# Two decoder layers on one core: the main products read their moving operand in blocks of 16 columns, last block first

## The chip, the cores and the metric

The kernel runs on one core of one Trainium2 chip. Its time is the device time of one execution in microseconds (us). Of the kernel before, three executions were timed: 1609.34, 1609.86 and 1611.76 us, median 1609.86 us.

## What is computed

Two layers of a causal decoder over 256 tokens of 1024 features, in float32. Each layer has a feed-forward half step, a group of parallel mixers, and a second feed-forward half step; a norm ends the whole.

```python
for l in range(DEPTH):
    h = _rmsnorm(x, ffn1_norm[l])
    x = x + 0.5 * _swiglu(h, ffn1_w_gate[l], ffn1_w_up[l], ffn1_w_down[l])
    h = _rmsnorm(x, mix_norm[l])
    hq, hf, hi, hg, s5_in, conv_in, att_in, gate_in = split(h @ w_in[l])
    y_a, y_b, y_c, y_d = hgrn2(...), s5(...), conformer_conv(...), dilated_attention(...)
    merged = sum_k sigmoid(gate_k) * (y_k @ w_branch[l, k])
    x = x + merged @ w_out[l]
    h = _rmsnorm(x, ffn2_norm[l])
    x = x + 0.5 * _swiglu(h, ffn2_w_gate[l], ffn2_w_up[l], ffn2_w_down[l])
return _rmsnorm(x, final_norm)
```

The weights of the large products (`w_gate`, `w_up`, `w_down`, `w_in`, `w_branch`, `w_out`, `s5_w_glu`) are float32 as well.

## The kernel before

**Products in three parts.** Every large product runs in the type float32r. Both factors are split exactly into a high and a low part: ScalarE copies the value into a float32r tile (`whi`, `hTh`, `gh`, ...), VectorE subtracts it from the value (`wlo`, `hTl`, `gl`, ...). `mm3` then adds three products into one bank of PSUM: high by high, high by low and low by high. All large products of the kernel go through `mm3`, and nothing else does; transposes, attention scores and the recurrences call `T.matmul` or `T.transpose` directly.

**What is stationary and what moves.** In the call `T.matmul(o, ah, bh)` the first factor is loaded into the array (a weight load of 128 columns), the second moves through it, and `o` is the output in PSUM. In `cols_tok` and in the down product the activations are stationary (128 tokens) and 512 columns of weights move: 512 columns a product. In `cols_feat` and `rows_feat` 128 columns of weights are stationary and the activations of all 256 tokens move: 256 columns a product. The moving operand is always a contiguous run of one partition's row, and so is the output.

**Shares of the work.** A down product accumulates over 22 blocks of 128 rows, the products of `cols_tok` and `cols_feat` over 8, those of `rows_feat` over 4. Four banks (`acc`) take the accumulations in turn; four others (`mx`) serve transposes and side work.

**Order.** Weights come by `Stream` in the order of their use: SyncE loads them into `raw` (4 buffers), ScalarE makes `whi`, VectorE `wlo` (5 slots ahead). Side work (the recurrences, attention, convolution, tables) is a list of generators, of which `tick` runs steps between the main products when the class `Paced` estimates that the engines have room. The estimate counts the elements of an access, `math.prod(ap.shape[1:])`, and so does not depend on how they are ordered. Every engine's call passes through one line of `Paced` (L72), so the profile gives line 72 for all of them, and the tiles tell the products apart: `gate_h`, `up_h`, `pgt_h`, `pu_h`, `pf_h`, `pq_h`, `pa_h`, `pb_h`, `br` and `glu` have 256 moving columns, `down`, `att_t`, `gate_t`, `up_t`, `po_t`, `pi_t` and `pg_t` have 512. `hl` and `as` are side work in plain float32 (the first recurrence, attention scores).

Of the kernel before, what the change touches and what calls it, by code (L numbers as in the profile page):

```python
# [28 lines left out]
NW, NRAW = 5, 4                # buffers of the weights' low parts (one more of the high ones), of their loads  # L29
NHEAP, NHALF = 23, 10          # working tiles of 4 KB and of 2 KB a partition  # L30
TAIL, LAST = 5, 2              # weights of a down product that are held for the other tokens; by halves of the columns
EARLIER, HELD = 1, 1           # how long before a phase's end the first tokens' rows are turned, loads are left alone
GO = -1
HOP, EARLY = 0.15, -0.3        # from one engine to another; how soon before its operands are there a step is issued
LAG, TABLE_LAG, LAST_LAG = 3.8, 2.0, 1.8   # how far side work, tables, convolution may put an engine behind
# [7 lines left out]
class Paced:  # L43
    """An engine's instructions, with an estimate of when each of them ends: in order, after the
    other engines' work on the same tiles."""
# [40 lines left out]

SETS = {AF.Exp: 1, AF.Tanh: 1, AF.Silu: 2, AF.Sin: 2, AF.Sigmoid: 3, AF.Ln: 4, AF.Gelu_apprx_tanh: 5}


class ActCost:  # L90
    """With the loads of the functions' tables."""
# [22 lines left out]
class Stream:  # L114
    """Weights in the order of their use: loads, then an exact split into two 12-bit parts.

    A group is (loads, slots): loads are (source, blocks of 128 rows), slots (load, view -> part of it)."""
# [36 lines left out]
    def pump(self, n=1, ahead=True):  # L154
        """The low part of a slot whose high part is there, then the high part of the next."""
        for _ in range(n):
            self.load()
            if self.n_high == self.n_split:
                self.high()
            if self.n_high == self.n_split or self.n_split - self.n_done >= NW:  # L160
                return
            i, src, hv = self.half
            lo = self.pool.tile([P, 1024], FR, tag="wlo", name=f"wlo{self.n_split}", bufs=NW)
            lv = lo.rearrange("p (k f) -> p k f", k=src.shape[1])
            self.dve.tensor_tensor(lv, src, hv.bitcast(F32), op=ALU.subtract)
            self.ready.append((hv, lv))
            self.n_split += 1
            self.left[i] -= 1
            if not self.left[i]:
                del self.raw[i]  # L170
            self.load()
            if ahead:
                self.high()
# [15 lines left out]
def trunk(ctx, tc, x_in, positions, ffn1_norm, ffn1_w_gate, ffn1_w_up, ffn1_w_down, mix_norm, w_in,  # L189
# [44 lines left out]
    def g_tok(w, pieces, n_loads=2):  # L234
        """512 columns in 2 or 4 loads; slots of 256 rows."""
        loads = []
        k = 8 // n_loads
        for i in range(n_loads):
            parts, at = [], 0
            for c0, n in pieces:  # L240
                parts.append((rows_of(w, P * k * i, P * k, c0, n), at, n))
                at += n
            loads.append((parts, k))
        groups.append((loads, [(i, lambda r, j=j: r[:, 2 * j:2 * j + 2, :]) for i in range(n_loads)
                               for j in range(k // 2)]))

    def g_feat(w, c0, n=512):
        """n columns; slots of 512 rows and 256 columns."""
        if n == 512:
            loads = [([(rows_of(w, 512 * i, 512, c0, 512), 0, 512)], 4) for i in range(2)]  # L250
            groups.append((loads, [(i, lambda r, j=j: r[:, :, 256 * j:256 * j + 256])
                                   for j in range(2) for i in range(2)]))
        else:
            loads = [([(rows_of(w, 0, 1024, c0, 256), 0, 256)], 8)]
            groups.append((loads, [(0, lambda r, j=j: r[:, 4 * j:4 * j + 4, :]) for j in range(2)]))

    def g_rows_feat(w, order):
        """512 rows, 1024 columns; slots of all rows and 256 columns, given by the first columns of their halves."""
        for h in range(2):
            (a, b), (c, d) = order[2 * h:2 * h + 2]  # L260
            cols = [a, b, c, d]
            parts = []
            i = 0
            while i < 4:
                j = i + 1
                while j < 4 and cols[j] == cols[j - 1] + 1:
                    j += 1
                parts.append((rows_of(w, 0, 512, P * cols[i], P * (j - i)), P * i, P * (j - i)))
                i = j
            groups.append(([(parts, 4)], [(0, lambda r, j=j: r[:, :, 256 * j:256 * j + 256]) for j in range(2)]))  # L270
# [24 lines left out]
    def by_head(pieces):  # L295
        """Pairs of heads' pieces: (pair, which of it, head, kind, first group, number of pairs)."""
        a = 0
        while a < len(pieces):
            k, h, g = pieces[a]
            n = 2 if a + 2 < len(pieces) and pieces[a + 2][0] == k else 1  # L300
            for e in range(2):
                yield a // 2, e, h + e, k, g, n
            a += 2 * n
# [28 lines left out]
    side = []  # L332

    def start(gen, late=0):
        """late: done after the others. A step ends with GO where the next one waits for no other engine."""
# [28 lines left out]
    def grab(n=1):  # L364
        """Banks of the side work's own, held over several steps."""
        while free[0] < n:
            yield
        free[0] -= n
# [47 lines left out]
    # rows of 128 features, turned into columns of scalars  # L416
# [45 lines left out]
    def masks():  # L462
        # the attention's masks: d = t - s
# [14 lines left out]
    def prepare():  # L478
        # the recurrence's masks: s in the left block whose right neighbour has t
# [10 lines left out]
        # columns  # L490
# [22 lines left out]
        # rotary tables  # L513
# [8 lines left out]
        # cos(a) = sin(pi/2 - |reduced a|)  # L522
# [11 lines left out]
        # the gates' lower bounds: softmax over the two layers, less its first part  # L534
# [13 lines left out]
        # S5: the discretized states of both layers, 128 states a column  # L548
# [24 lines left out]
        # mag - 1, by tanh where it is small  # L573
# [31 lines left out]
    # S5 of a layer: blocks of 4 tokens, t = 4 n + i; groups of 16 channels G = 16 jp + 2 jh + g,  # L605
    # states on partitions (g, p) and columns j = 8 jp + jh, a block's inputs on partitions (jp, i, c)
# [5 lines left out]
    def s5_tables(l):  # L612
# [15 lines left out]
        # powers of the states' factors  # L628
# [23 lines left out]
        # the discretized inputs' matrices  # L652
# [8 lines left out]
        # a block's inputs to its last state  # L661
# [26 lines left out]
        # the outputs' matrices, for each token of a block  # L688
# [23 lines left out]
        # a block's inputs to its outputs: K_s = Re(C a^s b) for a distance of s tokens, and d at 0  # L712
# [46 lines left out]
    def s5_turns(l):  # L759
# [5 lines left out]
        # e^{4 i theta n} by doubling  # L765
# [32 lines left out]
    def mm3(o, ah, al, bh, bl, first, last):  # L798
        T.matmul(o, ah, bh, start=first, stop=False)
# [3 lines left out]
    def cols_tok(hT, evac, name, outer=False, between=None, before_last=None, at=4, mid=True):  # L803
        """512 columns, tokens on partitions; outer: all of the first 128 tokens, then the others."""
# [44 lines left out]
    def cols_feat(hT, evac, name, n=512, quiet=False):  # L849
        """n columns on partitions, all tokens: evac(half, bank) with two blocks of 128 columns a bank."""  # L850
# [17 lines left out]
    def rows_feat(yT, evac, name):  # L868
        """1024 columns on partitions from 512 inputs: evac(i, bank), two blocks of 128 columns a bank."""
# [24 lines left out]
    class Norm:  # L894
        """The rows of a norm, turned into hT; the first tokens' before the last ones are there."""
# [9 lines left out]
        def square(self, t, h):  # L905
            """A half of the columns of x."""
# [111 lines left out]
    class Tail:  # L1018
        """What follows the last product of a phase: x += scale * acc, and the next norm."""
# [15 lines left out]
    def mixers(l, norm, tail, g_tab):  # L1035
# [131 lines left out]
        def s5():  # L1167
# [5 lines left out]
            # channel (q, h, c) of rows (h, c): q = 2 jp + a, and group 8 a + h of jp  # L1173
# [49 lines left out]
            # the blocks' last states, turned back  # L1223
# [99 lines left out]
        def rope_turn(raw, pieces, name):  # L1323
            """The first 32 of each head's 128 are rotated, then the heads turned onto partitions."""
# [45 lines left out]
        def attend(h):  # L1370
# [5 lines left out]
            for qb in range(2):  # L1376
# [34 lines left out]
                # probabilities onto key partitions  # L1411
# [220 lines left out]
```

## Time and profile before

| | |
|---|---|
| three timed executions | 1609.34, 1609.86, 1611.76 us |
| profiled execution, first to last instruction | 1609.4 us |
| TensorE busy | 1583.1 us, 98% |
| weight loads (beside the products) | 1442.8 us, 90% |
| VectorE busy | 1109.6 us, 69% |
| ScalarE busy | 837.6 us, 52% |
| moved by DMA | 282.48 MB, mean 176 GB/s |

The profiled execution spans 1609.4 us, 0.5 us below the median of the timed ones. Matmuls are pipelined: a record of a product begins when the one before it is still running, so the busy time of one record is longer than the distance from one start to the next. How fast a run of products goes is therefore read from the chain of waits in order of time, where a run of products is one row with its length and its count. The granted clock stands at full speed in all 40 slices of the page.

### The profile page before, as it was taken

What the parts mean: (1) busy time and instruction counts of PE and PEld (TensorE: products, weight loads), DVE (VectorE), ACT (ScalarE), POOL (GpSimd) and SP (SyncE); (2) the same over time, 40 slices, a digit from 0 to 9 for tenths busy, and PEclk for the clock granted to TensorE, in tenths of its full rate; (3) what the DMA queues carried; (4) which work ended last, traced back from release to release, by engine and by line L of the source; (5) the groups of instructions that cost most, each with busy time, mean ns of one, the idle gap of its engine ahead of it and who ended that gap; (6) DMA issues with size and microseconds to landing.
All of it is one profiled execution on the core that took longest, in us unless ns stands there. A gap on an engine that the chain in (4) does not pass through costs nothing.

```text
span 1609.4 us, 27748 instructions
## 1 busy us (share of the span) xinstructions
PE 1583.1 (98%) x11471; PEld 1442.8 (90%) x11471; DVE 1109.6 (69%) x1806; ACT 837.6 (52%) x1195; POOL 23.9 (1%) x53
## 2 busy tenths in 40 slices
PE   7999999999999999999999999999999999999998
PEld 6999788789899997999889988987899999989986
DVE  6778865876778866555478774567867898665553
ACT  5445455557565465444345544646565555654442
POOL 1000000000000000000000000000000000000000
PEclk9999999999999999999999999999999999999999
DMA  8565556444444456555555545664444545645551
GB/s 278 185 177 210 171 186 191 154 141 148 147 168 158 159 186 219 184 175 207 181 173 187 184 161 193 206 194 119 170 131 148 190 161 168 212 158 184 185 212 61
DMA packets 179519, 282.48 MB, mean 176 GB/s; under 512 B 26718, under 2 KB 82080, under 8 KB 179392
## 3 DMA queue, kind: packets, MB, share of 16 engines
q1 hardware_dynamic: 154240, 270.55, 49.7%
q10 hardware_dynamic: 24832, 9.97, 2.7%
q8 instruction: 90, 1.47, 0.4%
q14 instruction: 37, 0.30, 0.1%
q0 software_dynamic: 320, 0.18, 0.0%
HBM read 277.53 MB, written 3.15 MB: 174 GB/s over the span
## 4 chain that ended last, share of the span: by engine, by line
PE 94%; ACT 2%; DVE 2%; ACTq 1%; issue 1%; DMA 0%; SPq 0%; POOLq 0%; POOL 0%; DVEq 0%
PE down L72 15%; PE att_t L72 12%; PE up_h L72 12%; PE gate_h L72 12%; PE pgt_h L72 11%; PE br L72 6%; PE gate_t L72 3%; PE po_t L72 3%; PE up_t L72 2%; PE hl L72 2%; PE pi_t L72 1%; PE pa_h L72 1%; PE pb_h L72 1%; PE pg_t L72 1%; PE pq_h L72 1%; PE pf_h L72 1%
## 5 line engine op out<-in xcount | busy, mean ns | idle before, releaser
L72 DVE TENSOR_TENSOR wlo<-raw,whi 128x1024 fp32r<-128x1024 f32 x512 | 614.7, 1220 | 185.7 <-ACT whi L72 85.4
L72 ACT ACTIVATE whi<-raw 128x1024 fp32r<-128x1024 f32 x512 | 525.5, 1053 | 175.9 <-PE down L72 102.7
L72 PE MATMUL gate_h<-hTh,wlo 128*128 128x256 f32 x576 | 161.0, 280 | 2.8 <-DVE wlo L72 2.8
L72 PE MATMUL up_h<-hTh,wlo 128*128 128x256 f32 x576 | 160.9, 279 | 0.8 <-DVE wlo L72 0.8
L72 PE MATMUL gate_h<-hTh,whi 128*128 128x256 f32 x576 | 161.6, 280 | 0.0
L72 PE MATMUL up_h<-hTh,whi 128*128 128x256 f32 x576 | 161.1, 280 | 0.0
L72 PE MATMUL gate_h<-hTl,whi 128*128 128x256 f32 x576 | 160.4, 278 | 0.0
L72 PE MATMUL up_h<-hTl,whi 128*128 128x256 f32 x576 | 160.3, 278 | 0.0
L72 PE MATMUL pgt_h<-hTh,whi 128*128 128x256 f32 x512 | 145.6, 284 | 0.0
L72 PE MATMUL pgt_h<-hTh,wlo 128*128 128x256 f32 x512 | 142.6, 278 | 0.0
L72 PE MATMUL pgt_h<-hTl,whi 128*128 128x256 f32 x512 | 142.5, 278 | 0.0
L72 PE MATMUL down<-whi,gh 128*128 128x512 f32 x352 | 140.0, 398 | 0.0
L72 PE MATMUL down<-wlo,gh 128*128 128x512 f32 x352 | 139.2, 395 | 0.0
L72 PE MATMUL down<-whi,gl 128*128 128x512 f32 x352 | 139.1, 395 | 0.0
L72 PE MATMUL att_t<-whi,hTh 128*128 128x512 f32 x288 | 118.2, 410 | 0.0
L72 PE MATMUL att_t<-wlo,hTh 128*128 128x512 f32 x288 | 113.8, 395 | 0.0
L72 PE MATMUL att_t<-whi,hTl 128*128 128x512 f32 x288 | 113.8, 395 | 0.0
L72 PEld LDWEIGHTS gate_h<-hTh,wlo 128*128 128x128 f32 x576 | 108.1, 188 | 3.2 <-DVE wlo L72 3.2
L72 PEld LDWEIGHTS up_h<-hTh,wlo 128*128 128x128 f32 x576 | 108.1, 188 | 1.0 <-DVE wlo L72 1.0
L72 PEld LDWEIGHTS gate_h<-hTl,whi 128*128 128x128 f32 x576 | 108.3, 188 | 0.0
L72 PEld LDWEIGHTS up_h<-hTl,whi 128*128 128x128 f32 x576 | 108.3, 188 | 0.0
L72 PEld LDWEIGHTS up_h<-hTh,whi 128*128 128x128 f32 x576 | 107.8, 187 | 0.2
(375 smaller groups left out, 3357.7 us busy)
## 6 DMA issues: line engine op xcount, KB each, us to landing
raw<-in_w_in_dram SPq DMA_DIRECT2D x60, 1024.0 KB, 5.1
raw<-in_ffn_w_up_dram SPq DMA_DIRECT2D x44, 1024.0 KB, 5.2
raw<-in_ffn_w_down_dram SPq DMA_DIRECT2D x44, 1024.0 KB, 4.9
raw<-in_ffn_w_gate_dram SPq DMA_DIRECT2D x42, 1024.0 KB, 5.1
raw<-in_w_in_dram SPq DMA_DIRECT2D x72, 512.0 KB, 4.5
raw<-in_w_branch_dram SPq DMA_DIRECT2D x16, 1024.0 KB, 5.0
raw<-in_w_out_dram SPq DMA_DIRECT2D x8, 1024.0 KB, 5.0
raw<-in_s_w_glu_dram SPq DMA_DIRECT2D x16, 256.0 KB, 3.8
```

The lines of the kernel that those rows point to most:

```text
L72: return f(*args, **kw)
```

## The change

`mm3` passes its output and its two moving operands through a new function, `backwards`. It replaces the last dimension of an access (n columns, step 1) by two: n/16 blocks with a step of -16 columns, beginning at column n-16, and in each block 16 columns with step 1. The same columns meet the same output columns; the order over the columns is the last 16 in rising order, then the 16 before them, and so on. The stationary operands are as before. The rest of the diff takes out comments and docstrings; the line of `Paced` that all calls pass stays line 72.

```diff
+def backwards(ap):
+
+    dims = [list(d) for d in ap.ap]
+    step, n = dims[-1]
+    assert step == 1 and n % 16 == 0
+    return bass.AP(tensor=ap.tensor, offset=ap.offset + n - 16, ap=dims[:-1] + [[-16, n // 16], [1, 16]])
...
     def mm3(o, ah, al, bh, bl, first, last):
+        o, bh, bl = backwards(o), backwards(bh), backwards(bl)
         T.matmul(o, ah, bh, start=first, stop=False)
         T.matmul(o, ah, bl, start=False, stop=False)
         T.matmul(o, al, bh, start=False, stop=last)
```

On TensorE's queue the products keep their places. Before, in the first feed-forward phase (a gate product with 256 columns, then the change of weights from one slot to the next):

```order
L72 MATMUL gate_h_741<-hTl_0_113,whi_583 128x256
L72 MATMUL gate_h_741<-hTh_0_111,wlo_626 128x256
L72 MATMUL gate_h_741<-hTh_1_112,whi_628 128x256
L72 MATMUL gate_h_741<-hTl_1_114,whi_628 128x256
L72 MATMUL gate_h_741<-hTh_1_112,wlo_657 128x256
```

And the same place now:

```order
L72 MATMUL gate_h_741<-hTl_0_113,whi_583 128x16x16
L72 MATMUL gate_h_741<-hTh_0_111,wlo_626 128x16x16
L72 MATMUL gate_h_741<-hTh_1_112,whi_628 128x16x16
L72 MATMUL gate_h_741<-hTl_1_114,whi_628 128x16x16
L72 MATMUL gate_h_741<-hTh_1_112,wlo_657 128x16x16
```

Nothing has moved; each product has two dimensions of 16 where it had one of 256. The second place is where the mixers' first projections begin (`pi_t` is the projection whose 512 columns move, `xT` the transposes of the norm, `pu_h` the next projection, with 256 columns), with what each instruction waits for. Before:

```order
L72 MATMUL pi_t_2437<-whi_2388,hTl_1_2336 128x512
L72 MATMUL xT_10_2465<-ident,xn_1_2412 128x128 [waits DVE_49,PE_49]
...
L72 MATMUL pi_t_2438<-whi_2388,hTl_1_2336 128x512
L72 MATMUL pu_h_2524<-hTh_0_2333,whi_2422 128x256
L72 MATMUL pu_h_2524<-hTl_0_2335,whi_2422 128x256
```

And now:

```order
L72 MATMUL pi_t_2437<-whi_2388,hTl_1_2336 128x32x16
L72 MATMUL xT_10_2465<-ident,xn_1_2412 128x128 [waits DVE_49]
...
L72 MATMUL pi_t_2438<-whi_2388,hTl_1_2336 128x32x16
L72 MATMUL pu_h_2524<-hTh_0_2333,whi_2422 128x16x16 [waits PE_49]
L72 MATMUL pu_h_2524<-hTl_0_2335,whi_2422 128x16x16
```

Again no instruction has moved, but a wait of TensorE on its own semaphore (an earlier product's end) has gone from a transpose and come to the first product of a bank. On the other engines the order is the same, instruction by instruction.

## Rows read from the trace of the kernel before

**Rows 1.** The page: busy time, slices of 1/40 span, chain by engine.

```profile
PE 1583.1 (98%) x11471; PEld 1442.8 (90%) x11471; DVE 1109.6 (69%) x1806; ACT 837.6 (52%) x1195; POOL 23.9 (1%) x53
...
PEclk9999999999999999999999999999999999999999
...
PE 94%; ACT 2%; DVE 2%; ACTq 1%; issue 1%; DMA 0%; SPq 0%; POOLq 0%; POOL 0%; DVEq 0%
```

**Rows 2.** TensorE's waits: us in total, times, longest us.

```profile
PE xT L72 <- DVE xn L72: 8.8, 1, 8.8
PE gate_h L72 <- DVE wlo L72: 2.8, 2, 2.1
PE hd L72 <- ACT ak L72: 2.4, 2, 1.2
```

**Rows 3.** Product groups by form, TensorE: count, busy us and mean ns, idle before.

```profile
L72 PE MATMUL gate_h<-hTh,whi 128*128 128x256 f32 x576 | 161.6, 280 | 0.0
...
L72 PE MATMUL pgt_h<-hTh,whi 128*128 128x256 f32 x512 | 145.6, 284 | 0.0
...
L72 PE MATMUL down<-whi,gh 128*128 128x512 f32 x352 | 140.0, 398 | 0.0
...
L72 PE MATMUL att_t<-whi,hTh 128*128 128x512 f32 x288 | 118.2, 410 | 0.0
...
L72 PE MATMUL po_t<-whi,mTh 128*128 128x512 f32 x64 | 25.5, 398 | 0.0
...
L72 PE MATMUL pa_h<-hTh,whi 128*128 128x256 f32 x64 | 18.4, 288 | 0.0
...
L72 PE MATMUL pi_t<-whi,hTh 128*128 128x512 f32 x32 | 12.8, 401 | 0.2
...
L72 PE MATMUL as<-ak,aq 128*128 128x256 f32 x48 | 11.7, 379 | 0.0
```

**Rows 4.** The chain in order of time, long pieces: start us, length us, what.

```profile
50.81 10.88 PE up_h L72 x96
61.69 10.88 PE gate_h L72 x96
...
667.06 11.31 PE gate_h L72 x96
...
746.21 59.47 PE down L72 x255
...
944.41 59.47 PE down L72 x255
...
1379.39 10.88 PE br L72 x96
...
1518.09 11.31 PE up_h L72 x96
```

**Rows 5.** The same chain, pieces of side work from 345 us.

```profile
345.39 1.73 PE hl L72 x16
...
349.01 1.40 PE att_t L72 x6
...
365.46 1.29 PE as L72 x6
```

**Rows 6.** Three stretches: us, busy us by engine, granted clock, DMA share, GB/s.

```profile
50.10:94.90 44.80, 44.80 (x398) 44.80 (x397) 34.45 (x98) 23.26 (x34) 0.16 (x2) 1.00 0.62 197
655.80:739.40 83.60, 83.60 (x712) 83.60 (x711) 45.12 (x46) 37.69 (x45) 0.00 (x0) 1.00 0.54 185
756.30:789.90 33.60, 33.60 (x145) 27.07 (x144) 14.72 (x12) 12.74 (x12) 0.00 (x0) 1.00 0.55 188
```

**Rows 7.** Instructions in time from 667 us, weight loads: start us, length us.

```profile
667.02 0.19 PEld L72 LDWEIGHTS gate_h<-hTh,wlo 128*128 128x128 f32 x1
667.14 0.19 PEld L72 LDWEIGHTS gate_h<-hTh,whi 128*128 128x128 f32 x1
```

**Rows 8.** The same stretch, products.

```profile
667.02 0.28 PE L72 MATMUL gate_h<-hTl,whi 128*128 128x256 f32 x1
667.14 0.28 PE L72 MATMUL gate_h<-hTh,wlo 128*128 128x256 f32 x1
```

## The prediction, made before the changed kernel ran

> **What bounds the kernel now.** I read the page first: TensorE is busy for 98% of the span, it makes 94% of the chain that ended last, and its clock is granted in full in every slice [rows 1]. Its waits come next: the longest single one is 8.8 us at the start, where it waits for the first norm, and the others are 3 us and less in total [rows 2]. So the time is the pace of TensorE's products, and no other engine is late. VectorE, the next busy one, works for 34.45 of 44.80 us in its denser stretch [rows 6], 77%.
>
> How many products there are comes from the groups by form [rows 3]. With 256 moving columns: six groups of 576 (gate and up), three of 512 (`pgt_h`) and thirty of 64 (like `pa_h`), together 3456 + 1536 + 1920 = 6912. With 512 columns: three of 352 (`down`), three of 288 (`att_t`), nine of 64 (like `po_t`) and six of 32 (like `pi_t`), together 1056 + 864 + 576 + 192 = 2688. All of them are changed.
>
> Their pace comes from the chain in order of time. The 256-column products have two paces: 10.88 us for 96 is 113.3 ns each, 11.31 us for 96 is 117.8 ns each [rows 4]. Both are steady over dozens of products, and both occur for the same tiles (`gate_h` at 61.69 us and at 667.06 us). Of the chain's pieces of 84 or more such products, from the first at 50.81 us to the last at 1518.09 us, 936 products run at the first pace and 2748 at the second, a quarter and three quarters; the mean is 116.7 ns. The 512-column products have one pace, 59.47 us for 255, 233.2 ns [rows 4], and the short pieces among side work show the same, 1.40 us for 6 [rows 5]. By these the changed products take 6912 x 116.7 ns + 2688 x 233.2 ns = 807 + 627 = 1434 us of the 1609.4.
>
> What would these paces be if nothing were lost? Two rows of side work give floors [rows 5]. `hl` moves only 64 columns but loads 128 stationary ones each time: 1.73 us for 16 records, 108.1 ns, so a weight load alone can follow the next at that distance. `as` has 48 records of 256 plain float32 columns [rows 3] for the 24 such products of the code, so each of the two passes of a product takes 1.29 / 6 = 215.0 ns. I take that as the time of 512 column steps: at the upper of the clock's two levels, 2.4 GHz, they make 213.3 ns. Against these floors a 256-column product loses 5.2 or 9.7 ns, and a 512-column product 18.2 ns.
>
> What takes these? Not the clock: it is 1.00 in a stretch of either pace, and DMA is busier in the faster one (0.62 against 0.54) [rows 6]. Two streams read SBUF for TensorE at once: each product begins together with the weight load for the next (667.02 and 667.14 us in both views) [rows 7, 8]. That one instruction on the same tiles has two steady paces says that the loss depends on how the two streams lie to each other, not on what is computed. That is my reading; no row shows the collision itself.
>
> **The change, part by part.** (1) No instruction is added or moved on any engine's queue. Loads, splits, evacuations and side work keep their order, so the whole effect is in the pace of the 9600 products.
>
> (2) Some waits of TensorE on its own earlier products appear (at `pu_h`, for instance) and others go. The bank of such a product is one of four in turn, so its earlier use lies dozens of products back, several us at 113.3 ns or more: cost nothing. Were that cover gone, each would cost at most the length of a product's record, 0.28 us [rows 8]; with some fifteen such places that is 4 us.
>
> (3) The new order of the two streams. The trace has no operand with two dimensions, so I bound it from both sides. Gain, at most: all losses go, (116.7 - 108.1) x 6912 + (233.2 - 215.0) x 2688 = 59.4 + 48.9 = 108 us. Loss: at each block's edge the address jumps by 31 columns backwards. There are 6912 x 16 + 2688 x 32 = 196,608 blocks; if each edge costs one column step, 0.417 ns at the granted clock, this is 82 us. Between these ends I take the row that is nearest, the same instruction at its better pace: the new order shifts how the streams meet, three quarters of the 256-column products go from 117.8 to 113.3 ns (5184 x 4.5 ns = 23.3 us), and a 512-column product, twice the columns, to 226.6 ns (2688 x 6.6 ns = 17.7 us). The sum is 41 us. The span goes from 1609.4 to 1568.4 us; the median lies 0.5 us above that execution's span, so 1569 us.
>
> What is late next? With products 3% faster VectorE's 77% becomes 79%, and of TensorE's waits on it only the few that are there now should grow. I cost that at nothing; if the 2.8 us of `gate_h` [rows 2] doubled, it would be 3 us.
>
> The Trainium skill, TensorE: Matmul & The Clock Gate, section Back-to-back issue gap, puts a warm product at N / 2.4 + 2.5 ns, which for 256 and 512 columns is an estimate of 109.2 and 215.8 ns. The trace differs: 113.3 or 117.8 ns and 233.2 ns [rows 4]. By that rule the products have no loss that an order could give back, and the sum would be nothing; by the rows it is 41 us.
>
> **The rivals.** *The order is invisible* (no change). If the loss comes from how the reads share a port in time, or from a pattern of addresses that repeats within 16 columns, the order of whole blocks changes nothing, and within a block the reads are as before. For it: the paces don't depend on which tile moves, since weights and activations both show the loss [rows 4]. Against it: a loss that two paces show to be movable. Time: 1609.9 us.
>
> *All losses go.* The streams no longer meet at all: 1609.9 - 108 = 1502 us. Against it: the 512-column products show one pace everywhere, so a state without loss has never been hit by chance.
>
> *A jump costs at each edge* (slower). The place is the read of the moving operand, or the write of the output, at the end of each block of 16 columns. One column step an edge makes 1609.9 + 82 = 1692 us. It decides from very little: 3.2 us, which is 0.2%, is one lost step in 26 blocks. For it: nothing in the trace has such an access, so nothing shows it free. Against it: no instruction is added, and a run of 16 float32 values is long.
>
> *The worse pace everywhere* (a little slower). Products now at 113.3 ns go to 117.8 ns and nothing else changes: 1728 x 4.5 ns = 7.8 us, 1618 us. For it: which pace a stretch falls into is not steered by anything in the code.
>
> *The output no longer in one run* (much slower). If writing in blocks halves the pace, a 256-column product takes the 215.0 ns that `as` shows and a 512-column one twice that: (215.0 - 116.7) x 6912 + (430.0 - 233.2) x 2688 = 679 + 529 = 1208 us more, 2818 us. Against it: 16 columns of float32 in one run are a long way from single values. The Trainium skill, Advanced Engine Details and Errata, section PSUM Cachelines, speaks for this rival: any access that is not contiguous slows matmuls significantly; its next sentence asks only that every two consecutive elements be contiguous, which holds here. No run here shows either yet.
>
> **How the numbers follow.** Forecast (a better pace) 0.38, with a range of its own from 1540 to 1597 us, that is gains of 13 to 70 us; all losses go 0.06; invisible 0.31; worse pace everywhere 0.08; a jump at each edge 0.15; half pace 0.02. A measurement of this kernel can tell about 0.2%, 3.2 us, from no change. Faster is 0.38 + 0.06 = 0.44, same 0.31, slower 0.08 + 0.15 + 0.02 = 0.25. The range is 1530 to 1660 us: it leaves out the case in which all losses go (0.06), the dearer two thirds of the jumps at each edge (0.10) and half pace (0.02), 0.18 in all.
>
> **What would show it.** In the changed kernel's chain in order of time, a run of 96 products with 256 columns should take about 10.9 us throughout, and 255 `down` products about 57.8 us; counts, waits and the granted clock should stay. If the pieces read 10.88, 11.31 and 59.47 again, the order is invisible. Pieces well over 11.31 and 59.47 in the ratio 1 to 2 per product are the jump at each edge. Pieces near 10.4 and 54.8 mean that all losses went. If the pace is better but the span is not, the time has gone into new waits on VectorE or ScalarE, and my step (3) was right about the products but wrong about what hides behind them.

## The result: slower by 1.6%, at a pace that the trace of before did not have

The changed kernel takes 1634.93 us (median of 4 runs, 1633.76 to 1635.76), the kernel before 1609.60 us in the same comparison (1607.78 to 1611.76). The ratio is 1.0156, with an interval from 1.0139 to 1.0173. The forecast was 1569 us, so the direction was wrong; the time lies inside the stated range of 1530 to 1660 us. The profiled execution took 1633.76 us, its span is 1632.0 us, 22.6 us more than the 1609.4 us of before.

I read the same views in the same order. First the page of the changed kernel: busy time by engine, the granted clock in 40 slices, and the shares of the chain that ended last.

```profile
PE 1607.8 (99%) x11471; PEld 1463.7 (90%) x11471; DVE 1111.7 (68%) x1806; ACT 837.2 (51%) x1195; POOL 23.9 (1%) x53
...
PEclk9999999999999999999999999999999999999999
...
PE 95%; ACT 2%; DVE 1%; ACTq 0%; issue 0%; DMA 0%; SPq 0%; POOL 0%; POOLq 0%; DVEq 0%
```

Every count is that of [rows 1], the clock is granted in full as before, and TensorE makes 95% of the chain instead of 94%. Nothing was added and no clock was lost; TensorE itself is longer by 24.7 us.

TensorE's waits in the changed kernel: us in total, times, longest.

```profile
PE xT L72 <- DVE xn L72: 8.5, 1, 8.5
PE hd L72 <- ACT ak L72: 2.4, 2, 1.2
PE rt L72 <- DVE att L72: 1.7, 2, 0.9
PE gate_h L72 <- DVE wlo L72: 1.1, 1, 1.1
```

The wait of `gate_h` for the split has fallen from 2.8 to 1.1 us [rows 2], and no new one stands at the top. So the time is not in waits. The chain in order of time (start us, length us, what) shows where it is.

```profile
62.49 11.52 PE gate_h L72 x96
...
676.72 11.52 PE gate_h L72 x96
...
757.36 60.06 PE down L72 x255
...
957.35 60.04 PE down L72 x255
...
1398.39 11.52 PE br L72 x96
...
1539.59 11.52 PE up_h L72 x96
```

The two paces of 256-column products in [rows 4] have become one, and it is worse than both: 11.52 us for 96 is 120.0 ns each, against 113.3 and 117.8. The 512-column products went from 233.2 to 60.06 / 255 = 235.5 ns. The side work, which the change does not touch, keeps its pace: the chain among side work again.

```profile
349.17 1.73 PE hl L72 x16
...
352.81 1.41 PE att_t L72 x6
...
369.35 1.29 PE as L72 x6
```

`hl` and `as` are as in [rows 5], to the hundredth of a microsecond. So TensorE is not slower as such, only the changed products are.

Does this account for the whole difference? I summed, over all records of changed products, the time from each one's start to the next start on TensorE. For 256 columns it is 820.7 us before and 838.1 us after (+17.4), for 512 columns 639.7 and 645.0 us (+5.3). Together that is 22.7 us, and the spans differ by 22.6 us. All of it is pace. By the same records one fifth of the 6912 256-column products before, 1381, began 113 to 115 ns before the next one, and 5365 began 117 to 119 ns before it; the others are at waits and side work.

The same two stretches as in [rows 6] show it from the other side (us, busy us and instructions by engine, granted clock, DMA share, GB/s).

```profile
50.10:94.90 44.80, 44.80 (x376) 44.80 (x375) 33.98 (x93) 23.30 (x35) 0.16 (x2) 1.00 0.59 189
655.80:739.40 83.60, 83.60 (x699) 83.60 (x698) 43.35 (x42) 36.01 (x43) 0.00 (x0) 1.00 0.57 189
```

TensorE is busy throughout in both, at a clock of 1.00, but gets through 376 products instead of 398, and 699 instead of 712. Do not look for this in the mean length of a record: the group `gate_h<-hTh,whi` has 286 ns a product now and 280 before [rows 3], since records of pipelined products overlap, and a record is more than twice as long as the distance between two of them. The pace is read from the chain.

### The profile page after: what moved, and what is told of

The parts are those of the page before. It is cut to its first block, busy times and chain, and to the rows that moved or that the text cites. A ratio compares the mean times of both kernels' runs of the same rounds, so it can differ in the third digit from the quotient of the medians.

```text
span 1632.0 us, 27757 instructions
## 1 busy us (share of the span) xinstructions
PE 1607.8 (99%) x11471; PEld 1463.7 (90%) x11471; DVE 1111.7 (68%) x1806; ACT 837.2 (51%) x1195; POOL 23.9 (1%) x53
## 4 chain that ended last, share of the span: by engine, by line
PE 95%; ACT 2%; DVE 1%; ACTq 0%; issue 0%; DMA 0%; SPq 0%; POOL 0%; POOLq 0%; DVEq 0%
PE down L72 15%; PE gate_h L72 12%; PE up_h L72 12%; PE att_t L72 12%; PE pgt_h L72 11%; PE br L72 6%; PE up_t L72 3%; PE gate_t L72 3%; PE po_t L72 3%; PE hl L72 2%; PE pi_t L72 1%; PE pa_h L72 1%; PE pb_h L72 1%; PE pf_h L72 1%; PE pq_h L72 1%; PE glu L72 1%
## 5 line engine op out<-in xcount | busy, mean ns | idle before, releaser
L72 PEld LDWEIGHTS gate_h<-hTh,whi 128*128 128x128 f32 x576 | 108.3, 188 | 0.1
```

The lines of the kernel that those rows point to most:

```text
L72: return f(*args, **kw)
```

## The experiments

Four theories were tried. **A, edges:** each jump at the end of a block of the moving read costs something. **B, output:** writing the output in blocks costs. **C, falling order:** reading from high to low addresses costs. **C2, place:** what counts is at which place the moving read stands, within 64 columns (256 bytes), when the stationary read of the next weight load stands at its own place; order and alignment both only change that relation. Paces below come from the chains of the experiments, as above; spans are to be held against 1609.4 (before) and 1632.0 (after). Except where an interval is given each is one profiled execution. Eleven executions of the kernel before, timed beside two of the experiments, took 1602.92 to 1613.98 us, so a difference in span under some 11 us shows nothing by itself; what decides are the paces, each of which repeats to a few hundredths of a microsecond over the pieces of 96 products.

**Which half of the change?** In `mm3`, against the changed kernel:

```diff
-        o, bh, bl = backwards(o), backwards(bh), backwards(bl)
+        bh, bl = backwards(bh), backwards(bl)      # e1_read_only
+        o = backwards(o)                           # e2_write_only
```

> Only the two moving operands are read in blocks of 16 from the last to the first; the output is written in one run as before, so the columns of every main product come out permuted and the result is not the reference's. Theory A (each edge between blocks in the read costs): the paces of the changed kernel, 11.52 us for 96 products of 256 columns and 60.05 us for 255 of 512, span 1632 us. Theory B (the output in blocks costs): the paces of the kernel before, 10.88 or 11.31 and 59.47, span 1609 us. Theory C (the order against the weight load, read behind the moving operand): as A.

> Only the output is written in blocks of 16 from the last to the first, the moving operands are read in one run; columns come out permuted, so the result is not the reference's. Theory A (edges in the read): the paces before, span 1609 us. Theory B (edges in the output): 11.52 and 60.05 us, span 1632 us. Theory C (order of the read against the weight load): the paces before, 1609 us.

Span 1632.6 us for the read alone, 1608.2 us for the output alone. Chain of the read alone:

```profile
62.68 11.52 PE gate_h L72 x96
...
757.38 60.06 PE down L72 x255
...
1540.26 11.52 PE up_h L72 x96
```

And of the output alone:

```profile
61.59 10.88 PE gate_h L72 x96
...
746.13 59.47 PE down L72 x255
...
1516.90 11.31 PE up_h L72 x96
```

The read alone has the paces of the change, the output alone those of [rows 4]. B falls: an output written in blocks of 16 columns costs nothing that shows. All that follows is about the read.

**The edges without the falling order.** Blocks of 16 columns that begin 12 columns apart, so that each edge is a jump of 3 columns back, as many edges as in the change, in rising order:

```diff
-    return bass.AP(tensor=ap.tensor, offset=ap.offset + n - 16, ap=dims[:-1] + [[-16, n // 16], [1, 16]])
+    return bass.AP(tensor=ap.tensor, offset=ap.offset, ap=dims[:-1] + [[12, n // 16], [1, 16]])
```

> The moving operands are read in rising blocks of 16 columns, each beginning 12 columns after the last one, so there are as many edges as in the change but hardly a jump, and the order rises; the output is one run. Some columns are read twice and the last quarter never, so the result is not the reference's. Theory A (an edge of the access costs, whatever the direction): 11.52 us for 96 and 60.05 us for 255, span 1632 us. Theory C (the falling order costs by how it meets the weight load): the paces before, 10.88 or 11.31 and 59.47 us, span 1609 us. Theory B (output): the paces before.

Span 1607.8 us. Chain:

```profile
62.24 11.28 PE gate_h L72 x96
...
746.65 59.38 PE down L72 x255
...
944.30 58.68 PE down L72 x255
```

The 256-column products take 117.5 ns, one pace throughout, and `down` 232.9 or 230.1 ns in its two stretches. As many edges as in the change and no loss: A falls in its plain form. That the 256-column products have one pace instead of two is a hint that the order matters in another way.

**The same fall in larger blocks.** Blocks of 64 columns, read and output, from the last to the first:

```diff
-    assert step == 1 and n % 16 == 0
-    return bass.AP(tensor=ap.tensor, offset=ap.offset + n - 16, ap=dims[:-1] + [[-16, n // 16], [1, 16]])
+    assert step == 1 and n % 64 == 0
+    return bass.AP(tensor=ap.tensor, offset=ap.offset + n - 64, ap=dims[:-1] + [[-64, n // 64], [1, 64]])
```

> The change with blocks of 64 columns in place of 16, read and output alike. Theory A (edges): a quarter of the edges; if a 256-column product is 106.7 ns and 16 edges of 0.83 ns, 4 edges make 110.0 ns, 10.56 us for 96, and the span falls under the one before, to about 1570 us, unless a floor of the weight load holds it at 108 ns; if the edges come on top of the loss that was there, between 11.31 and 11.52 us, span 1609 to 1632 us. Theory C (order): as the change, 11.52 and 60.05 us, span 1632 us. Theory B (output): as A.

Span 1608.9 us, and the paces of before exactly:

```profile
62.31 10.88 PE gate_h L72 x96
...
747.20 59.47 PE down L72 x255
...
1517.59 11.31 PE up_h L72 x96
```

Under C2 it must be so, since falling by 64 columns leaves every place within 64 columns as it was; under A and C it could still be that a quarter of the edges costs too little to see. The next pair takes these apart.

**Falling, but rising within 64; and the reverse.** Only the 256-column products, read alone. Blocks of 16 in steps of -48 columns fall in address, but their place within 64 columns rises (0, 16, 32, 48), as before. Steps of +48 rise in address, and their place falls, as in the change.

```diff
+    if n != 256:
+        return ap
-    return bass.AP(tensor=ap.tensor, offset=ap.offset + n - 16, ap=dims[:-1] + [[-16, n // 16], [1, 16]])
+    return bass.AP(tensor=ap.tensor, offset=ap.offset - ap.offset % 1024 + 768, ap=dims[:-1] + [[-48, 16], [1, 16]])  # e5_fall48
+    return bass.AP(tensor=ap.tensor, offset=ap.offset - ap.offset % 1024 + 48, ap=dims[:-1] + [[48, 16], [1, 16]])    # e6_rise48
```

> Only products with 256 columns are changed, in the read alone: 16 blocks of 16 columns that begin 48 columns before the last one, from column 768 of the tile down to 48. The order falls and each edge is a jump of 63 columns, but taken modulo 64 columns the blocks come in rising order, as before. It reads other columns than it should, so the result is not the reference's. Theory C2 (what counts is the place within 64 columns, 256 bytes, as the blocks of 64 suggest): the paces before, 10.88 or 11.31 us for 96, span 1609 us. Theory A (each jump between blocks of 16 costs): 11.52 us or more, span 1627 us or more. Theory C (falling order costs): 11.52 us, 1627 us.

> As the one before, but the blocks begin 48 columns after the last one, from column 48 up to 768: the order rises, and modulo 64 columns the blocks come in falling order, as in the change. Other columns are read than should be, so the result is not the reference's. Theory C2 (place within 64 columns): the change's pace, 11.52 us for 96, span 1627 us. Theory C (falling order): the paces before, 1609 us. Theory A (each jump): 11.52 us or more.

Spans 1604.8 us and 1630.6 us. Chain of the falling one:

```profile
62.33 10.88 PE gate_h L72 x96
...
226.19 11.31 PE pu_h L72 x96
...
746.70 59.47 PE down L72 x255
```

And of the rising one:

```profile
63.07 11.52 PE gate_h L72 x96
...
758.50 59.47 PE down L72 x255
...
1538.82 11.52 PE up_h L72 x96
```

The falling one has the two paces of before, the rising one the 120.0 ns of the change, and `down`, which neither touches, stays at 233.2 ns. (That the falling one's span is under that of before is no gain of its order: it has the same two paces, but more stretches at the better one, 2287 products at 113 to 115 ns against 1381.) Both have the same number of edges. C falls, A falls for good, and of the four theories C2 is left: the place within 64 columns.

**The kernel before, with only the place shifted.** If the relation of the two reads is what counts, moving the weights against the activations must change the pace with no order changed at all. One unused tile is allocated between the working tiles and the split weights; 16 columns are 64 bytes a partition.

```diff
+    G.memset(const([P, 16], "pad"), 0.0)           # e8_pad64; [P, 8], [P, 32], [P, 48] in e11, e9, e10
     S.activation(tiny([P, 1], "warm", 1), neghalf, AF.Silu)
```

> The kernel before with 64 unused bytes a partition between the working tiles and the split weights, set to zero once by GpSimd, so that stationary and moving operands lie 64 bytes (16 columns) otherwise to each other within 256 bytes; nothing else changes and the result is the reference's. Theory C2 (the two streams of reads meet by their places): paces other than 10.88, 11.31 and 59.47 us, in either direction, span anywhere from 1560 to 1640 us. Theory A (cost in the moving stream alone): the paces before, 1609 us.

> The kernel before with 128 unused bytes between working tiles and split weights (64 bytes gave 12.00 ns more or less per product by kind). The result is the reference's. Theory C2 (the relation of the two streams within 256 bytes sets the pace): a third set of paces, for 256 columns between 113.3 and 120.0 ns, for 512 between 226 and 236 ns, and not those of 64 bytes (120.0 and 227.3). If only the step from aligned to unaligned counted (rival): the paces of 64 bytes again, 120.0 and 227.3 ns, span 1615 us.

> As before with 192 bytes, which brings the weights to the working tiles' place less 64 bytes the other way. The result is the reference's. Theory C2 with a period of 256 bytes: again another set of paces within 113.3 to 120.0 and 226 to 236 ns; since moving and stationary change sides between the two kinds of product, what 64 bytes did to the 512-column products (faster) may now come to the 256-column ones. Rival (aligned or not): 120.0 and 227.3 ns.

> As before with 32 bytes. The result is the reference's. Theory C2 with memory lines or banks of 64 bytes: paces between those of the kernel before (113.3 and 117.8; 233.2 ns) and those of 64 bytes (120.0; 227.3). If what counts is 64-byte blocks alone: those of one of the two.

Spans 1615.0, 1587.5, 1619.4 and 1608.5 us, for 64, 128, 192 and 32 bytes. Chain with 64 bytes:

```profile
62.23 11.52 PE gate_h L72 x96
...
751.00 57.96 PE down L72 x255
```

With 192 and with 32 bytes the first line reads 11.40 and 11.20 us, the second 59.22 and 59.51 us. The 64 bytes alone, in the kernel before and in its own order, give the 120.0 ns of the change, while `down` gets better, 227.3 ns; there it is the weights that move and the activations that are stationary, so the same pad shifts the two the other way. 128 bytes gain 22 us, of which more below.

Two of the four expectations were met only in part. For 128 bytes a third set of paces was expected for both kinds of product. (Its "12.00 ns more or less" for 64 bytes is a slip: that pad had made a 256-column product 2.2 to 6.7 ns slower and a 512-column one 5.9 ns faster.) Only the 512-column products got a new pace, 228.9 and in places 232.7 ns; the 256-column ones went on at the 113.3 and 117.8 ns of before, differently shared out. And for 192 bytes the 256-column products might have gained what the others gained with 64; they got slower, 118.7 ns in most stretches and 120.0 in the rest. The rival, aligned or not, fell: 64, 128 and 192 bytes do not give one and the same set.

**Is it the stationary read itself?** A pad also shifts the weights against everything else that reads or writes them. So two more kernels. In one no tile moves; the stationary operand of the 256-column products alone is read 16 columns (64 bytes) further on (48 back at a row's end, which is the same place within 64), so that other weights are multiplied. In the other the pad stands ahead of all tiles, so that everything moves by 64 bytes together.

```diff
+    by = 16 if at + n + 16 <= row else -48         # e13: place of the stationary read
+    return bass.AP(tensor=ap.tensor, offset=ap.offset + by, ap=dims)
...
+        if size(bh) == 256:
+            ah, al = backwards(ah), backwards(al)
```

> Only the stationary operands of the products with 256 moving columns are read 16 columns (64 bytes) further on (48 back at a row's end); no tile is moved, moving operands and outputs are as before. The wrong weights are read, so the result is not the reference's. If the stationary read is the second stream: the 256-column products behave as with 64 bytes of padding, 11.52 us for 96, the 512-column ones as before, 59.47 for 255, span about 1628 us. If the places of the tiles count by themselves, or another engine's accesses are the second stream: the paces before, 10.88, 11.31 and 59.47 us, span 1609 us.

> 64 unused bytes ahead of all tiles, so that working tiles and split weights are shifted alike and keep their relation. The result is the reference's. If the relation of the two streams counts: the paces before, 10.88, 11.31 and 59.47 us, span 1609 us. If places count by themselves: other paces, like those with 64 bytes between (11.52 and 57.95 us).

Spans 1627.9 and 1609.5 us. Chain with the stationary read shifted:

```profile
62.86 11.52 PE gate_h L72 x96
...
756.11 59.49 PE down L72 x255
...
1536.20 11.52 PE up_h L72 x96
```

And with all tiles shifted together:

```profile
61.76 10.88 PE gate_h L72 x96
...
747.80 59.47 PE down L72 x255
...
1518.17 11.31 PE up_h L72 x96
```

The first has 120.0 ns although every tile lies where it lay; the second has exactly the paces of before although every tile has moved. So the place of a tile by itself does not make the pace. Nor do the accesses of the other engines: the 120.0 ns of the change comes from the order of the moving read alone (e1), the same 120.0 ns here from the place of the stationary read alone, and in the changed kernel the pace is the same in a stretch in which VectorE works for 33.98 of 44.80 us and in one in which it works for 43.35 of 83.60. What is left is how the moving and the stationary read of TensorE lie to each other. For the loss of the change C2 is shown.

**The change with its loss taken back.** The changed kernel with the 64-byte pad:

> The changed kernel (blocks of 16, last first, read and output) with 64 unused bytes between working tiles and split weights. The result is the reference's. Theory C2: the order costs by how it meets the weight load, so with other places the same order can be faster than the kernel before: not 120.0 and 235.4 ns, a span anywhere from 1560 to 1632 us. Theory A (a jump between blocks of 16 costs by itself, on top): 120.0 ns or more for 256 columns whatever the places, and the span at 1630 us or more.

Span 1613.6 us. Chain:

```profile
62.30 11.31 PE gate_h L72 x96
...
749.52 59.50 PE down L72 x255
```

That is 117.8 and 233.3 ns, one pace each. The order of the change and all its edges are there, yet 18 of its 22.6 us are gone.

**A version that is faster.** Reversing in blocks of 32 swaps the halves of every 64 columns, which by C2 is the same as a shift of 128 bytes; the 128-byte pad does that without any change of order.

```diff
-    assert step == 1 and n % 16 == 0
-    return bass.AP(tensor=ap.tensor, offset=ap.offset + n - 16, ap=dims[:-1] + [[-16, n // 16], [1, 16]])
+    assert step == 1 and n % 32 == 0
+    return bass.AP(tensor=ap.tensor, offset=ap.offset + n - 32, ap=dims[:-1] + [[-32, n // 32], [1, 32]])  # e7, e15
```

> The change with blocks of 32 columns, read and output alike. Theory C2 with a period of 64 columns: the same sequence as before but begun half a period later, so a steady pace between 10.88 and 11.52 us for 96, not the 11.52 of the change; with a period of 32 columns exactly the paces before, 10.88 and 11.31. Theory A (each jump costs, but four in a product are hidden): eight jumps, half way, about 11.4 us and a span of 1618 us.

> Blocks of 32 columns, last first, timed. By the one run before: 1594 us, a ratio to the kernel before near 0.990; an interval that holds 1 would show that the single run was chance.

> The kernel before with 128 bytes between working tiles and split weights, timed. By the one run before: 1589 us, a ratio near 0.987. Theory C2 takes a shift of 128 bytes for the same as blocks of 32 columns, so both should be equal but for which stretches fall into which of the two paces.

> Blocks of 32 columns, last first, and 128 bytes of padding between working tiles and split weights in one kernel. The result is the reference's. Theory C2 with a period of 256 bytes: two shifts by 128 bytes cancel, so the paces of the kernel before come back, 10.88 and 11.31 us for 96 and 59.47 us for 255, span 1609 us, though each alone is faster. If the two gains had different causes they would stay or add up: span 1590 us or less.

The single execution of blocks of 32 (e7) had a span of 1592.2 us. Timed, over six executions, blocks of 32 take 1598.92 us (ratio 0.9929, 0.9904 to 0.9953), the pad of 128 bytes, over five, 1584.82 us (ratio 0.9853, 0.9830 to 0.9876). So the pad is faster by 1.5% and the blocks by 0.7%, both clear of noise, but they are not equal. Chain of the pad, profiled with the timed runs:

```profile
61.21 10.88 PE gate_h L72 x96
...
735.64 58.37 PE down L72 x255
...
1493.61 10.88 PE up_h L72 x96
```

Chain of the blocks of 32, likewise (e15):

```profile
62.24 11.31 PE gate_h L72 x96
...
661.74 11.31 PE gate_h L72 x96
...
740.89 59.35 PE down L72 x255
```

And of the same kernel in its other profiled execution (e7), at the same place:

```profile
660.91 10.88 PE gate_h L72 x96
```

Over two profiled executions each, both kernels have the same set of paces, 113.3 (113.6 in places) or 117.8 ns and 228.9 or 232.7 ns, as two forms of one shift should by C2. What differs is the share: in the long pieces of the chain 2928 of 3588 256-column products with the pad ran at about 113.3 ns, and 384 of 3684 with the blocks (in e7 1140 of 3684).

This share C2 does not explain, and the larger part of the gain comes from it. By the records, from start to start, the pad (e16) took 8.6 us from the 512-column products, which have a new pace, and 18.1 us from the 256-column ones, which have the two paces of before: 5254 of 6912 of them at 113 to 115 ns instead of 1381. The two rows of `gate_h` above are one kernel, so every tile lies at the same address in both, and yet the pace is 113.3 ns in one execution and 117.8 in the other. So which of these two paces a stretch takes is not settled by how the two reads lie to each other in address.

The expectation for blocks of 32 (e7) had one steady pace between the two for a period of 64 columns, and exactly the paces of before for a period of 32. For the 256-column products the second came. That the pattern as a whole does not repeat at 32 columns (128 bytes) is seen in the 512-column products, 228.9 ns against 233.2, and in the 256-column ones between pads of 64 and 192 bytes, 120.0 ns against 118.7 in most stretches.

Both shifts together (e17) have a span of 1614.8 us, and `gate_h` at 63.01 us takes 11.31, `down` at 751.00 us 59.48 us: the two gains cancel, and the paces are among those of before. That every long 256-column stretch would then fall into the slower of the two was not foreseen; only 180 of 6912 products are at 113 to 115 ns, against 1381 before.

All that was measured, for the read order of before (rising) and of the change (falling within 64 columns), by how far the weights are shifted:

| order, shift | ns per 256-column product | ns per 512-column product | span, us |
|---|---|---|---|
| rising, 0 | 113.3 / 117.8 | 233.2 | 1609.4 |
| rising, 32 bytes | 116.7 | 233.3 | 1608.5 |
| rising, 64 bytes | 120.0 | 227.3 | 1615.0 |
| rising, 128 bytes (pad) | 113.3 / 117.8 | 228.9 / 232.7 | 1582.9 |
| rising, 192 bytes | 118.7 / 120.0 | 232.2 | 1619.4 |
| falling, 0 (the change) | 120.0 | 235.5 | 1632.0 |
| falling, 64 bytes | 117.8 | 233.3 | 1613.6 |

## Why the prediction was wrong

**What bounds the kernel** was right: the time is the pace of TensorE's products, and the pace accounts for all of the 22.6 us (22.7 by the starts).

**Step (1), nothing is added or moved,** was right: all counts of the page are unchanged.

**Step (2), waits on its own products cost nothing,** was right: none is among the waits of the changed kernel, its longest three beside the start are 2.4 us and less in total, and e2, which has the blocks of the output, stands at 1608.2 us.

**Step (3), the new order of the two streams,** failed, and with it the forecast. Its reading that the loss depends on how the two streams lie to each other was right, as e13 and e14 show. The evidence given for it was not, and there it was luck: "one instruction on the same tiles has two steady paces" happens with every address unchanged, as the two executions of the blocks of 32 show (e7 and e15), so the two paces do not tell two relations of the reads apart. What failed is the choice between the bounds, which rested on that. I took "the row that is nearest, the same instruction at its better pace", as if the two paces in the trace were all there are and a new order could only pick the better one. Another relation can have paces of its own; this one's is 120.0 ns, 2.2 ns worse than the worse pace and 6.7 ns worse than the better. The term was a gain of 41 us, 23.3 from the 256-column products and 17.7 from the others, and measured as a loss of 22.7 us, 17.4 and 5.3.

By nothing in the trace was the sign known: two paces show that the loss varies, not which way a new order moves it. From two bounds of -108 and +82 us, with no row between that has another relation of the two reads, the middle is 13 us, far nearer to nothing than to 41. That the measured time lies inside the range is luck too: its upper part stood for a cost at each edge, and that is not what came. Paces like the forecast's exist, though: 113.3 ns in most stretches and 228.9 ns with the 128-byte pad, 227.3 ns with the 64-byte one, where 113.3 and 226.6 were forecast.

**What is late next:** nothing, as forecast, though for a product that got slower.

The rivals. *The order is invisible* failed where it supposed a pattern "that repeats within 16 columns": the pattern repeats at 64 (e4, e5), so blocks of 16 do change it, and blocks of 64 would have made this rival right. *A jump costs at each edge* had the sign and not the cause: e3, e5 and e12 have as many edges and no such loss, and its price of 82 us was nearly four times the loss. Its mark, "pieces well over 11.31 and 59.47 in the ratio 1 to 2 per product", did not hold either: 120.0 is 2.2 to 6.7 ns over, 235.5 only 2.3. *The worse pace everywhere* came nearest in kind, one pace instead of two, but at 117.8 ns it is 1618 us; the pace that came was not in the trace. *All losses go* is far off too: with none of the relations tried did the products come near 108.1 and 215.0 ns; the best are 113.3 and 227.3. *The output no longer in one run* cost nothing that shows (e2, 1608.2 us). On that the Trainium skill, Advanced Engine Details and Errata, section PSUM Cachelines, says two things, that access which is not contiguous slows matmuls significantly, and that every two consecutive elements should be contiguous; the measurement agrees with the second and not with the first, for blocks of 16. The formula N / 2.4 + 2.5 ns, which the prediction took from the Trainium skill, TensorE: Matmul & The Clock Gate, section Back-to-back issue gap, is given there for an isolated product; of a stream of weight loads and products the section says that both set the spacing. So "no loss that an order could give back" did not follow from it.

## What to carry to other kernels

Where TensorE bounds a kernel and loads new weights for every product, shift one of the two operands by 64, 128 and 192 bytes with an unused tile and read the pace from the chain: here that is one line, and 128 bytes gave 1.5%. Time several executions: about two thirds of that gain is a larger share of stretches at a pace that the kernel already had, and what sets this share is not known. Forecast nothing for a new order from paces that the trace shows for the old one: two paces prove that something varies, not that the new order moves it, nor where to. And take an effect apart by halves first (read or write), then by a pair that has equal edges and opposite order.

## What the runs showed of the hardware

The pace of a product depends on how its moving read and the weight load beside it lie to each other in address, and the pattern repeats with 256 bytes a partition: blocks that keep every place within 256 bytes keep every pace (e4, e5), moving all tiles together keeps them too (e14), and moving the stationary read alone by 64 bytes makes 120.0 ns of 113.3 or 117.8 (e13). The Trainium skill, SBUF — State Buffer, section Who interferes with whom, lists TensorE's two SBUF read ports, for the moving operand and for the weight load, as independent, and says that only the port pair shared by VectorE and GpSimd causes contention. In time these runs differ: another relation of the two reads changes a product by up to 6.7 ns with 256 columns (113.3 to 120.0) and by 8.2 ns with 512 (227.3 to 235.5).

The direction of the read costs nothing in itself, nor do edges at every 16 columns (e5 has both and keeps 113.3 and 117.8 ns), nor does an output in blocks (e2 keeps these and 233.2 ns).

Three things stay open. Why just these relations give these paces: no run shows how the memory is divided. What picks 113.3 or 117.8 ns in a stretch: in none of the 51 unbroken stretches of 24 or more 256-column products in the trace of before does the pace change from one to the other, but the same kernel with blocks of 32 had 1140 of its 3684 products in long pieces at the better pace in one execution and 384 in another. And whether a shift other than 32, 64, 128 and 192 bytes, or one of its own for the 512-column products, which like 64 bytes best (227.3 ns), would give more: it wasn't tried.
